# mLSTM gates as 80 rows of one chunk each, and other instruction orders in the MLP and the key projections

## The chip, the cores and the metric

The kernel runs on one core of a Trainium2 chip. A core has five engines that each work through their own instruction stream in order: TensorE (PE, matrix products into eight PSUM banks of 128 x 512 float32), VectorE (DVE), ScalarE (ACT, functions of one operand), GpSimd (POOL) and SyncE (SP), from whose queue this kernel issues all its DMAs. [...] The metric is the device time of one execution in microseconds (us). The profile records one execution with every instruction's start and end; "granted clock" is the share of full speed at which TensorE's clock ran.

## The reference

A two-layer diffusion transformer on 1024 latent tokens of width 1024 and 256 context tokens, all in float32. In both layers each token is normalised (RMS), scaled and shifted by vectors from an AdaLN projection, goes through a mixer and then through an MLP with squared ReLU (width 4096). Layer 0's mixer joins a bidirectional mLSTM of four heads with a windowed attention of eight heads; layer 1's is a grouped-query attention with eight query and two key heads. The part that the change touches most are the mLSTM's gates, for each of 4 heads and 2 directions:

```python
def step(carry, inp):                     # over chunks of 128 tokens
    c_mat, n_vec, m = carry
    qc, kc, vc, ic, fc = inp              # ic input gate, fc log-sigmoid of forget gate
    bcum = jnp.cumsum(fc, axis=-1)
    d_log = jnp.where(lower, bcum[..., :, None] - bcum[..., None, :] + ic[..., None, :], -jnp.inf)
    inter_log = bcum + m[..., None]
    m_t = jnp.maximum(inter_log, jnp.max(d_log, axis=-1))
    inter_w = jnp.exp(inter_log - m_t)
    ...
    w_log = b_last[..., None] - bcum + ic
    m_new = jnp.maximum(b_last + m, jnp.max(w_log, axis=-1))
    carry_w = jnp.exp(b_last + m - m_new)
    w = jnp.exp(w_log - m_new[..., None])
```

The forward direction starts with the two context chunks and goes on with the eight latent ones; the backward direction takes the two context chunks in reverse, then the eight latent chunks in reverse. So there are 2 x 4 x 10 = 80 pairs of a row and a chunk. The running maximum m_t can be had from one scan, m_t = max(m_(t-1) + f_t, i_t), and the cumulative sum from another.

The MLP is `x + gate * (relu(h @ w1) ** 2 @ w2)` for both streams in layer 0, and for the latent tokens alone in layer 1.

## The kernel before, in words

**Number format and products.** Every operand of a large product is split in two parts, a rounded high part ("hi", fp32r) and the rest ("lo"), and a product is three matmuls: hi·hi, hi·lo, lo·hi. `split` (L376 to L379) does this with one copy on ACT and one subtraction on POOL or DVE. A projection of 512 tokens (`proj`, L408) is thus 24 matmuls of 512 columns.

**Who sets the order.** The program is traced in Python order. A planner then orders each engine's instructions: an instruction that its model finds ready goes ahead, earlier traced ones first. Inside `manual_schedule(engines=...)` the named engines keep the traced order. Tiles are recycled; the framework adds the waits that this takes.

**First stage of layer 0** (`first`, L2275, then `mixer0`, L1249). The tokens are normalised and the gate and key projections run as each part becomes ready. `swa_setup` (L1316) copies the gate projection to `gy` (L1329: rows 0 to 3 input gates forward, 32 to 35 input gates backward, 64 to 67 and 96 to 99 the forget gates), projects values (L1330), turns them by TensorE transposes (L1335), and normalises and rotates the keys by `qk_norm` (L470 to L482; single buffers qsq, qt, qsw, qrs). `gates` (L1150 to L1247) follows at once; then the first pair of queries, and seven projections of the gather (L1372 to L1387: mLSTM queries, keys, values, output gates, written to DRAM through the one tile `ev`), which use PSUM banks 6 and 7. Then the window attention (`swa`) with the rest of the gather as filler. Only the mLSTM, later, uses what `gates` returns: `mr` and `ir` (rows of 1280 in high and low parts: the running maximum less the cumulative sum, and the decay), `cb` (the decay of a whole chunk, on all partitions) and `tq` (three values per token, tokens on partitions).

`gates` before works on rows of 1280 tokens: the log-sigmoid on 64 partitions (L1161 to L1168), the backward rows turned around by copies (L1176 to L1182), two scans over 36 x 1280 (L1187, L1188), differences (L1190 to L1200), high and low parts (L1206 to L1210), and for each direction four exponentials into rows of a tile `q` (L1225, L1228), whose last columns are spread to all partitions by matmuls (L1237) and whose ten chunks are transposed (L1242) and copied (L1246).

**The MLP** (`mlp`, L485). Latent products are done by a scheme with seven products in place of eight (sums of blocks of both operands). The first half (`mlp_hidden`, L495) goes over 16 pairs of 128-wide rows of w1. `start` (L661) does pairs 0 and 1 while the normalisation still runs: a list `side` (L677) of steps (normalisation of the second latent group, ten; of the context, `norm_steps`, 17; sums of blocks, four) is advanced by `beside(n)` with counts from `turns` (L713, L734). PSUM banks of a rotating list "A" take the products. `pair` (L775) does one pair: seven products of 12 matmuls, in layer 0 also two context products (`direct`), sums on DVE (`tt`, L624), squared ReLU on ACT (L581, L582), stores to DRAM, and beside it, by `step`, the splits of the next pair's weights (`sums`, L538). In layer 0 `fill(k)` advances the AdaLN projection of layer 1 (`ada_sums`, L195), which sums on DVE (L209, L211) and ends with eight small matmuls (L220). The second half (`mlp_out`, L993) reads the stored sums and w2 in stages "14", "56", "27", "3"; in "14", each step b feeds product 1 (banks 0 to 3) and product 4 (banks 4 to 7). `ahead` (L841) loads and splits its first three steps during the last pair.

After the stages, layer 0 does the context's own second half: 32 steps of twelve matmuls into four banks, four copies on ACT (L1118, L1119), transposes (L1126) and the residual. Then `mixer1` (L1726) loads the weights of the two key heads and of the values, and runs `keys` (L1754: projection; squares and rotation; sum of squares by a matmul at L1772 and root; split) for three token groups and two heads, interleaved by hand (L1817 to L1826).

## Time and profile before

| | |
|---|---|
| median of three runs | 2866.45 us (2858.58 to 2867.11) |
| profiled execution | 2866.29 us, its span 2864.5 us |
| mean granted clock of TensorE | 0.983 |
| TensorE busy | 2733.7 us, 95% of the span |
| DVE, ACT, POOL busy | 1996.7, 1493.8, 1131.6 us |
| DMA | 427.87 MB, 149 GB/s over the span |

How to read the rows of the profile: a row of the waits is "engine, line, waited for: total us, times, longest us". A row of the groups is "line engine operation out<-in count | busy us, mean ns of one | idle us before it <- what ended it". A row of the timeline is "start us, length us, engine line operation", with the idle time before it and what ended it in brackets. A row of the windows is a stretch of the span, its length, the busy time of PE, PEld (TensorE's weight loads), DVE, ACT and POOL with the instructions counted in brackets, the granted clock, the busy share of the DMA engines and GB/s.

### The profile page before, as it was taken

What the parts mean: (1) busy time and instruction counts of PE and PEld (TensorE: products, weight loads), DVE (VectorE), ACT (ScalarE), POOL (GpSimd) and SP (SyncE); (2) the same over time, 40 slices, a digit from 0 to 9 for tenths busy, and PEclk for the clock granted to TensorE, in tenths of its full rate; (3) what the DMA queues carried; (4) which work ended last, traced back from release to release, by engine and by line L of the source; (5) the groups of instructions that cost most, each with busy time, mean ns of one, the idle gap of its engine ahead of it and who ended that gap; (6) DMA issues with size and microseconds to landing.
All of it is one profiled execution on the core that took longest, in us unless ns stands there. A gap on an engine that the chain in (4) does not pass through costs nothing.

```text
span 2864.5 us, 41088 instructions
## 1 busy us (share of the span) xinstructions
PE 2733.7 (95%) x14806; PEld 2314.0 (81%) x14806; DVE 1996.7 (70%) x3289; ACT 1493.8 (52%) x2624; POOL 1131.6 (40%) x748
## 2 busy tenths in 40 slices
PE   6789999999999999989999998999989999999999
PEld 3678788878788878868878888999988888888877
DVE  5836556567868887756777846888885567766766
ACT  5565554444564334334345645888876555444332
POOL 3431221110227666550000335777776398840000
PEclk9989999999999999999999999999999999999999
DMA  6112224252333466669764720100026245577674
GB/s 232 61 48 95 90 88 145 96 199 89 115 103 126 165 209 214 219 209 339 249 213 156 250 88 32 34 19 27 19 83 209 86 158 195 193 254 269 212 229 155
DMA packets 193965, 427.87 MB, mean 149 GB/s; under 512 B 20960, under 2 KB 46688, under 8 KB 193760
## 3 DMA queue, kind: packets, MB, share of 16 engines
q1 hardware_dynamic: 193760, 425.24, 44.7%
q8 instruction: 116, 1.90, 0.3%
q14 instruction: 89, 0.73, 0.1%
HBM read 322.65 MB, written 102.50 MB: 148 GB/s over the span
## 4 chain that ended last, share of the span: by engine, by line
PE 67%; DVE 13%; DMA 7%; issue 5%; ACT 4%; POOL 2%; SPq 0%; DVEq 0%; POOLq 0%; ACTq 0%
PE psum L1020 15%; PE psum L569 15%; PE psum L404 5%; PE psum L406 5%; PE psum L405 5%; PE psum L1955 4%; PE psum L2141 3%; DMA hhiraw<-in_w 3%; PE psum L1861 3%; DVE W L379 2%; PE psum L1111 2%; DVE F L211 2%; DVE F L624 1%; PE psum L1453 1%; POOL W L379 1%
## 5 line engine op out<-in xcount | busy, mean ns | idle before, releaser
L379 POOL TENSOR_TENSOR W<-F,W 128x512 fp32r<-128x512 f32 (+2 forms) x323 | 522.8, 1634 | 507.8 <-ACT W L378 390.7
L1020 PE MATMUL psum<-W,W 128*128 128x512 f32 x2688 | 617.1, 391 | 8.7 <-DVE W L379 5.2
L1020 PEld LDWEIGHTS psum<-W,W 128*128 128x128 f32 x2688 | 503.9, 188 | 121.4 <-DVE W L379 12.6
L569 PE MATMUL psum<-hhi,W 128*128 128x512 f32 (+1 forms) x1600 | 448.7, 360 | 12.8 <-DVE x L624 5.9
L378 ACT ACTIVATE W<-F 128x512 fp32r<-128x512 f32 (+2 forms) x380 | 274.2, 739 | 264.5 <-POOL F L542 96.9
L569 PEld LDWEIGHTS psum<-hhi,W 128*128 128x128 f32 x1600 | 288.9, 191 | 59.1 <-DVE x L624 7.2
L569 PE MATMUL psum<-hlo,W 128*128 128x512 f32 (+1 forms) x800 | 287.2, 359 | 0.0
L378 ACT ACTIVATE W<-hhiraw 128x1024 fp32r<-128x1024 f32 x98 | 104.0, 1061 | 320.9 <-PE psum L1020 247.3
L404 PE MATMUL psum<-hhi,W 128*128 128x512 f32 (+1 forms) x624 | 232.9, 373 | 6.7 <-DVE F L478 6.7
L406 PE MATMUL psum<-hhi,W 128*128 128x512 f32 (+1 forms) x624 | 227.8, 365 | 0.4 <-POOL W L379 0.4
L405 PE MATMUL psum<-hlo,W 128*128 128x512 f32 (+1 forms) x624 | 227.5, 365 | 0.0
L943 DVE TENSOR_TENSOR hhiraw<-hhiraw 128x512 f32<-128x512 f32 x154 | 104.8, 689 | 118.2 <-DMA hhiraw<-in_w 117.4
L542 POOL TENSOR_TENSOR F<-F 128x512 f32<-128x512 f32 x112 | 170.0, 1518 | 20.4 <-DMA F<-in_w 6.9
L569 PEld LDWEIGHTS psum<-hlo,W 128*128 128x128 f32 x800 | 153.3, 192 | 21.8 <-issue 0.2
L372 POOL TENSOR_TENSOR hlo<-F,hhi 128x512 fp32r<-128x512 f32 (+1 forms) x24 | 27.9, 1165 | 358.8 <-ACT F L371 353.7
L379 DVE TENSOR_TENSOR W<-hhiraw,W 128x1024 fp32r<-128x1024 f32 x98 | 119.6, 1221 | 50.0 <-ACT W L378 49.8
L404 PEld LDWEIGHTS psum<-hhi,W 128*128 128x128 f32 x624 | 119.0, 191 | 27.6 <-DVE F L478 7.1
L406 PEld LDWEIGHTS psum<-hhi,W 128*128 128x128 f32 x624 | 118.7, 190 | 17.9 <-POOL W L379 0.8
L405 PEld LDWEIGHTS psum<-hlo,W 128*128 128x128 f32 x624 | 119.2, 191 | 16.9 <-issue 1.7
L569 PE MATMUL psum<-x,W 128*128 128x512 f32 x504 | 123.5, 389 | 0.0
L581 ACT ACTIVATE F<-F 128x512 f32<-128x512 f32 x82 | 51.2, 625 | 134.7 <-DVE F L624 134.7
L379 DVE TENSOR_TENSOR W<-hloraw,W 128x1024 fp32r<-128x1024 f32 x98 | 119.4, 1219 | 1.6 <-ACT W L378 1.6
(435 smaller groups left out, 6471.5 us busy)
## 6 DMA issues: line engine op xcount, KB each, us to landing
F<-in_w SPq DMA_DIRECT2D x104, 512.0 KB, 4.3
hloraw<-hd SPq DMA_DIRECT2D x90, 512.0 KB, 4.8
hhiraw<-in_w SPq DMA_DIRECT2D x72, 512.0 KB, 3.9
hd<-F SPq DMA_DIRECT2D x142, 256.0 KB, 2.1
hhiraw<-in_w SPq DMA_DIRECT2D x116, 256.0 KB, 5.3
F<-in_ada_w SPq DMA_DIRECT2D x96, 256.0 KB, 3.2
hd<-x SPq DMA_DIRECT2D x90, 256.0 KB, 2.4
F<-in_win SPq DMA_DIRECT2D x33, 512.0 KB, 3.7
```

The costliest lines, as they stand in the source:

```text
L378: nc.scalar.activation(hi, src, AF.Copy)
L379: eng.tensor_tensor(lo, src, hi.bitcast(F32), op=ALU.subtract)
L404: nc.tensor.matmul(ps, sh, mh, start=i == 0, stop=False)
L405: nc.tensor.matmul(ps, sh, ml, start=False, stop=False)
L406: nc.tensor.matmul(ps, sl, mh, start=False, stop=i == n - 1)
L542: add = lambda o, p, q, how: nc.gpsimd.tensor_tensor(o, p, q, op=how)
L569: nc.tensor.matmul(ps, w[i][:, p], B[j][k], start=first and j == 0 and m == 0, stop=last and j == 3 and m == 2)
L943: tt = lambda o, p, q, how: eng.tensor_tensor(o, p, q, op=how)
L1020: nc.tensor.matmul(bank(base + i), A[u][:, p], B[v], start=first and m == 0, stop=last and m == 2)
L1861: nc.tensor.matmul(ps, s[:, c], m[:, j, t0 : t0 + QT], start=j == 0 and i == 0, stop=j == ND - 1 and i == 2)
L1955: nc.tensor.matmul(u.o[:, :QT], v[x], p[y], start=c == 0 and m == 0, stop=c == 2 * NB - 1 and m == 2)
L2141: self.nc.tensor.matmul(ps, x[:, c], y, start=first and m == 0, stop=last and m == 2)
```

## The change

**Gates.** The four groups of gate rows are written to DRAM and read back as two tiles of 128 columns (input and forget gates), forward rows as partitions 0 to 39 (head by chunk), backward ones as 64 to 103. Everything then works on 128 columns. Scans run inside each chunk, the backward ones through a reversed view. The sum and the maximum of a whole chunk are one column; a matmul with this column as a broadcast stationary operand and the identity spreads it as a row to all partitions (`across`), where a scan over 80 values, ten per head and direction, carries the maximum from chunk to chunk (the first value of each head is set apart by NEG). It comes back as one column by a product with the identity and a sum along the row, and one more DVE instruction corrects the maxima inside the chunks. `mr` and `ir` go back to rows of 1280 through DRAM; `tq` takes three transposes. The call stands after the first queries and the seven gathered projections. Two tiles of 1280 columns are used where there were six.

```diff
+        gd = dr.tile([4, 4, T], F32, tag="gd", name="gd")
+        for i in range(4):
+            nc.sync.dma_start(gd[i], gy[32 * i : 32 * i + 4, :])
+        for i in range(4):
+            R = (FW, BW)[i % 2]
+            nc.sync.dma_start((ig, y)[i // 2][R, :], gd[i].rearrange("h (c t) -> (h c) t", t=P))
...
+        for R, o in ((FW, slice(None)), (BW, slice(None, None, -1))):
+            nc.vector.tensor_tensor_scan(b[R, o], z[R, :], f[R, o], 0.0, op0=ALU.mult, op1=ALU.add)
+            nc.vector.tensor_tensor_scan(m[R, o], f[R, o], ig[R, o], NEG, op0=ALU.add, op1=ALU.max)
...
+        def across(c):
+            ps = psp.tile("G", "gx")[:, :P]
+            nc.tensor.matmul(ps, col[:, c : c + 1].to_broadcast([P, P]), self.ident, start=True, stop=True)
+            return ps
+        for i, x in enumerate((t, kept)):
+            ps = across(i)
+            nc.vector.tensor_copy(x[:, 0:40], ps[:, 0:40])
...
+        nc.vector.tensor_tensor_scan(t[:, 0:80], t[:, 0:80], kept[:, 0:80], 0.0, op0=ALU.add, op1=ALU.max)
...
+        nc.vector.tensor_tensor(row, row, self.ident, op=ALU.mult)
+        nc.vector.tensor_reduce(c0, row, AX.X, ALU.add)
+        nc.vector.scalar_tensor_tensor(m, b, c0, m, op0=ALU.add, op1=ALU.max)
...
+        nc.scalar.activation(iw, M, AF.Exp, scale=-1.0, bias=c0)
+        nc.scalar.activation(ar, g, AF.Exp, bias=col[:, 3:4])
+        nc.scalar.activation(em, m, AF.Exp, scale=-1.0)
...
+        for i, (x, dst) in enumerate(((Mh, mr), (Ml, mr), (Ih, ir), (Il, ir))):
+            for d, R in enumerate((FW, BW)):
+                w = dr.tile([4, T], F32, tag=f"gd{i}{d}", name=f"gd{i}{d}")
+                nc.sync.dma_start(w.rearrange("h (c t) -> (h c) t", t=P), x[R, :].bitcast(F32))
+                r = 64 * d + 32 * (i % 2)
+                nc.sync.dma_start(dst[r : r + 4, :].bitcast(F32), w)
...
+        for k, x in enumerate((g, ar, em)):
+            nc.tensor.transpose(ps[:, k * P : k * P + P], x, self.ident)
...
-                mr, ir, cb, tq = self.gates(kp, small, psa, gy)
                 for _ in st[-1](psa, 0, qs):
                     pass
...
                 for _ in range(7):
                     next(heads[0])
+                mr, ir, cb, tq = self.gates(kp, small, psa, dr, gy)
```

**Start of the MLP.** `norm_apply` is cut in a first part (scale, shift, high part) and a second (low part). In layer 0 the context's normalisation does the first part of chunk j before the second part of chunk j-1, in 18 steps. The counts of `turns` change, the last context product no longer leaves one drain undone, and the list of banks after the start begins with 4 in layer 0.

```diff
+        for j in range(ND + 1):
+            if j < ND:
+                t.append(self.apply_first(g, ps, layer, which, tp, j, three))
+            if j:
+                self.apply_second(g, layer, which, j - 1, t[j - 1], three)
             yield
...
-                turns = iter((1, 1, 1, 1, 1, 1, 4, 4) if ctx else (0, 1, 1, 2, 1, 2, 1, 2))
+                turns = iter((1, 1, 1, 2, 2, 2, 2, 3) if ctx else (0, 1, 1, 2, 1, 2, 1, 2))
...
-                turns = iter((2, 7, 1, 1) if ctx else (1, 1, 1, 1))
+                turns = iter((4, 6, 1, 1) if ctx else (1, 1, 1, 1))
...
-                        one_left(1)
+                        one_left(int(f < 3))
...
-            psp.tags["A"] = [[0, 1, 2, 3, 4, 5, 6] + ([] if ctx else [7]), 0]
+            psp.tags["A"] = [[4, 5, 6, 0, 1, 2, 3] if ctx else list(range(8)), 0]
```

**End of the first half, start of the second.** In the last pair the AdaLN step moves from behind the first product to behind the third, as in the other pairs. `ahead` loads two steps later where there is a filler. The last two pairs, in both layers, keep the traced order on all engines and on SP. In stage "14" the first two steps are taken together: product 1 of both, product 4 of the first, then (at b = 1) product 4 of the second.

```diff
-            if b == NFF // 2 - 1:
-                fill(2)
...
-            if b < NFF // 2 - 1:
-                fill(3)
+            fill(3)
...
+            if filler:
+                yield
+                yield
             for k in range(2):
                 feed.load(k)
...
-            pair(b, A, nxt)
+            if b < NFF // 2 - 2:
+                pair(b, A, nxt)
+            else:
+                with self.tc.manual_schedule(engines={E.PE, E.DVE, E.Activation, E.Pool, E.SP}):
+                    pair(b, A, nxt)
...
+                if stage == 0 and b < 2:
+                    if b == 0:
+                        first_two = [(*w, e, *queue[e]) for w in plan[kind] for e in range(2)]
+                    queue.popleft()
+                    work = first_two[3:] if b else first_two[:3]
```

**Keys.** The loads and splits of layer 1's first weights are issued from `mlp_out`: those of the keys before the four copies of the context's result, those of the values behind them, with ACT in that order. For each group and head the sum of squares of the group before comes ahead of the next projection; for the context group each head's sum of squares comes ahead of a value product.

```diff
+        wk, wv = self.first_weights
+        wk()
+        with self.tc.manual_schedule(engines={mybir.EngineType.Activation}):
+            for (half, i, k), y in zip(parts, ys):
+                nc.scalar.activation(y, bank(k), AF.Copy)
+            wv()
...
-                    for i in (g, g - 1, g, g - 1):
+                    for i in (g - 1, g, g, g - 1):
                         next(ks[i][kv])
             for kv in range(NKV):
+                next(ks[2][kv])
                 vals(TGS[1], (kv,))
-                for _ in range(2):
-                    next(ks[2][kv])
+                next(ks[2][kv])
```

More of the change, by code (lines that the diff above doesn't have):

```diff
@@ L858, in ahead @@
             yield
-            yield
-            yield
+            if not filler:
+                yield
+                yield
             for k in (1, 2):
@@ L1079, in mlp_out @@
                     both = kind == "3"
-                    first = b == 0 and not (both and half == R)
+                    first = b + e == 0 and not (both and half == R)
                     last = b + e == ns - 1 and not (both and half == L)
@@ L1117, in mlp_out @@
         ys = cuts(F, H, *(3 * PG + i * H for i in range(4)))
-        for (half, i, k), y in zip(parts, ys):
-            nc.scalar.activation(y, bank(k), AF.Copy)
+        wk, wv = self.first_weights
[4 more added lines that the diff above has]
+            wv()
         for j, k in zip(range(0, ND, 2), (5, 2, 7, 6)):
@@ L1140, in norm_steps @@
         yield
-        for j in range(ND):
-            self.norm_apply(g, ps, layer, which, tp, [j], three)
+        if layer:
+            for j in range(ND):
+                self.norm_apply(g, ps, layer, which, tp, [j], three)
+                yield
+            return
+        t = []
+        for j in range(ND + 1):
[3 more added lines that the diff above has]
+                self.apply_second(g, layer, which, j - 1, t[j - 1], three)
             yield
@@ L1213, in gates @@
[L1213 removed]
         tq = cbt.tile([P, 2, NT, 12], F32, tag="tq")
+        ps = across(4)
         for d in range(2):
[L1216 to L1246 removed]
@@ L1723, in residual, with begin_mixer1, keys, vals @@
         self.nc.vector.scalar_tensor_tensor(xs, ps[:, :n], gate, xs, op0=ALU.mult, op1=ALU.add)
+    def begin_mixer1(self):
+        a, wp = self.a, self.weights_ring((4, 5, 0, 1), (PG, 2 * PG, 0, 0))
+        self.wk, self.wv = [], []
+        def keys():
+            self.wk += [self.unit(wp, a["win1"][8 + kv]) for kv in range(2)]
+        def vals():
+            self.wv += [self.unit(wp, a["wv1"][:, i * 1024 : i * 1024 + 1024]) for i in range(2)]
+        self.first_weights = keys, vals
     def mixer1(self, xd, side):
```

176 lines of the change are left out of this document (76 added, 100 removed).

## The prediction

> **What bounds the kernel now.** I read the page's busy times first, then TensorE's waits, then windows and timelines around each long wait.
>
> ```profile
> span 2864.5 us, 41088 instructions
> PE 2733.7 (95%) x14806; PEld 2314.0 (81%) x14806; DVE 1996.7 (70%) x3289; ACT 1493.8 (52%) x2624; POOL 1131.6 (40%) x748
> ```
>
> TensorE (PE) is the bound: 2864.5 - 2733.7 = 130.8 us of the span is all that it idles. An edit that leaves its matmuls as they are can win only some of that idle time, and the slow clock that follows it. So the question for each edit is which PE wait it touches (columns: total, times, longest):
>
> ```profile
> PE psum L220 <- DVE F L211: 12.9, 3, 8.5
> PE psum L404 <- DVE F L478: 6.7, 1, 6.7
> PE psum L569 <- DVE x L624: 5.9, 3, 3.1
> PE psum L569 <- ACT F L581: 5.4, 1, 5.4
> PE psum L1772 <- DVE F L465: 4.6, 2, 3.1
> PE psum L1126 <- ACT F L1119: 4.4, 1, 4.4
> PE psum L1242 <- issue: 4.3, 1, 4.3
> PE psum L404 <- DVE F L1775: 3.6, 1, 3.6
> PE psum L1020 <- ACT F L581: 2.0, 1, 2.0
> PE psum L1413 <- DVE small L1246: 1.6, 1, 1.6
> PE psum L1020 <- DVE x L624: 1.2, 1, 1.2
> ```
>
> Windows around them (window, then its length, then busy time of PE, PEld, DVE, ACT, POOL, then the granted clock, DMA share, GB/s) price the waits with the clock:
>
> ```profile
> 92.50:191.00 98.50, 80.74 (x374) 64.75 (x374) 64.79 (x83) 61.47 (x94) 40.15 (x26) 0.88 0.16 52
> 93.00:147.00 54.00, 42.96 (x193) 34.14 (x192) 53.31 (x54) 34.57 (x52) 23.58 (x15) 0.91 0.17 55
> 142.00:146.00 4.00, 4.00 (x10) 3.13 (x11) 3.94 (x4) 3.89 (x6) 2.53 (x2) 0.50 0.25 99
> 872.00:876.00 4.00, 3.76 (x9) 2.99 (x10) 4.00 (x4) 3.43 (x9) 4.00 (x4) 0.50 0.05 6
> 1152.00:1156.00 4.00, 4.00 (x12) 3.15 (x13) 3.20 (x5) 2.18 (x4) 2.23 (x2) 0.66 0.98 334
> 1230.00:1252.00 22.00, 13.53 (x51) 10.96 (x50) 16.04 (x19) 10.13 (x19) 11.27 (x9) 0.77 0.56 180
> 1268.00:1282.00 14.00, 10.82 (x40) 8.18 (x39) 7.17 (x6) 7.09 (x11) 8.58 (x4) 0.88 0.99 367
> 1676.00:1680.00 4.00, 3.87 (x20) 3.74 (x21) 3.25 (x7) 1.86 (x5) 1.53 (x1) 0.63 0.38 95
> 1746.00:1750.00 4.00, 3.29 (x17) 3.29 (x18) 1.04 (x3) 0.42 (x1) 0.00 (x0) 0.65 0.29 114
> 2500.00:2555.00 55.00, 55.00 (x244) 45.43 (x243) 34.29 (x40) 26.55 (x41) 39.47 (x24) 1.00 0.61 202
> ```
>
> After a wait of some microseconds PE runs about 4 us at a clock of 0.5 to 0.66: 1.4 to 2 us more are lost. In the gates' stage VectorE (DVE) is busy 53.31 of 54 us. There, DVE and not PE sets the pace.
>
> **Part 1, the gates.** 92.5 is where the gate projections end, 191 where the first attention scores start. PE's work between them, at full clock, is about 80.74 x 0.88 = 71 us. The gates' own forms of that window:
>
> ```profile
> L1242 PE MATMUL psum<-ident,x 128*128 128x128 f32 x20 | 4.1, 354 | 4.3 <-issue 4.3
> L1237 PE MATMUL psum<-x,ident 128*128 128x10 f32 x16 | 2.8, 308 | 0.2 <-ACT x L1228 0.2
> L1165 DVE SCALAR_TENSOR_TENSOR x<-x,x 64x1280 f32<-64x1280 f32 x1 | 3.5, 3487 | 0.1
> L1187 DVE TENSOR_TENSOR_SCAN x<-s6f,x 36x1280 f32<-36x1280 f32 x1 | 2.8, 2817 | 0.0
> L1246 DVE COPY small<-psum 128x16 f32<-128x16 f32 x12 | 1.3, 166 | 0.6 <-PE psum L1242 0.6
> L379 DVE TENSOR_TENSOR VV<-psum,VV 128x128 fp32r<-128x128 f32 x2 | 0.6, 282 | 0.0
> L1182 DVE COPY x<-s6f 4x256 f32<-4x256 f32 x1 | 0.3, 283 | 0.0
> L1225 ACT ACTIVATE x<-x 4x1280 f32<-4x1280 f32 x4 | 5.1, 1266 | 7.0 <-DVE x L1188 7.0
> L1206 ACT ACTIVATE s6f<-x 4x256 f32<-4x256 f32 x1 | 0.4, 413 | 0.0
> ```
>
> Removed on DVE: 23 such forms (L1164 to L1246; the costliest and the last stand above), 40.7 us by their busy column. Removed on ScalarE (ACT): the forms L1161 to L1230, 22.8 us, first and last by size above. PE loses 36 instructions, 4.1 + 2.8 = 6.9 us, and gets three broadcast products and three transposes, 6 x 0.354 = 2.1 at most. Rows 1280 long become 128 long, so the new gates have about 48 DVE instructions between 0.166 and 0.282 us: 8 to 14, I take 11 (the scan, 2817/10 = 0.28, agrees with the upper row). ACT: nine of about 0.3, 3 us. Net relief: DVE 30 us, ACT 20, PE 5.
>
> [...]
>
> What this frees: L478 at 141.4 is what PE waits for 6.7 us, because the next gathered projection needs bank 6, which the last K tile holds, and L478 stands behind L1187, L1188, L1190, L1191, L1196 and L1200 on DVE. Without these six forms, none longer than L1187's 2.8 us, it comes up to 17 us sooner, before PE gets there. The wait at L1242 (4.3) and the one at L1413 (1.6, scores behind the gates' copies in bank 5) belong to the old gates. So the stage can shrink from 98.5 to 71 - 5 = 66 us and a little more: 32 us at best. What is late next: the K and Q chains through single buffers qsq, qt, qrs, whose POOL and ACT parts stay; and PE's own waits for the new gates, whose products are strung between DVE steps. PE has seven gathered projections to fill with. Bounds: 10 (only the named waits, 12.6, less some) and 28; I take **19**, nearer the upper, since DVE's saturation is the plain cause.
>
> Its DMAs: 24 on SP (4 + 4 in, 8 + 8 out), in write-read pairs through DRAM, among the gather's weight loads and stores.
>
> ```profile
> u<-F SPq DMA_DIRECT2D x16, 128.0 KB, 1.7
> ACT F L1381 <- DMA u<-F: 9.8, 3, 7.0
> 2554.68 25.55 PE L1020 MATMUL psum<-W,W 128*128 128x512 f32 x112
> ```
>
> Each read waits for its write, by the row 1.7 us; behind it on SP stand the stores u<-F, and for these waits ACT with its one tile ev. mr and ir themselves aren't read before the mLSTM. Cover: two PSUM banks of gather, two projections of 24 matmuls at 25.55/112 = 0.228, 5.4 us each. I cost them at nothing while SP is held for less than that at a time; more is the third rival.
>
> **Part 2, start of layer 0's MLP.** The 5.4 us wait for L581 is bank 0, still held by the context's first tile, whose drain stands behind the group sums on ACT:
>
> ```profile
> 860.89 0.68 DVE L624 TENSOR_TENSOR F<-psum,F 128x512 f32<-128x512 f32 x1
> 871.83 0.36 ACT L581 ACTIVATE F<-psum 128x256 f32<-128x256 f32 x1
> 872.24 0.80 PE L569 MATMUL psum<-hhi,W 128*128 128x512 f32 x1 [5.45 <-ACT F L581]
> ```
>
> The new order of banks starts with 4, drained at 861.6 by L624, then 5 and 6; bank 0 comes three products (8 us) later. The turns, the step-ahead in the normalisation and the empty drain list move work earlier: 32 steps in place of 31, no new instruction. Worth 5.45 + half of 3.76 = 7.3 at most, 3 if DVE (busy 4 of 4 us there) makes the later products wait; I take **6**.
>
> **Part 3, end of that MLP's first half.** The longest wait, 8.47 us before L220, is the last AdaLN product standing behind the pair's first product while L211 on DVE is unfinished; it moves two products (2 x 12 matmuls, 5.4 us) later, and the last two pairs follow program order, where L211 stands in the pair before it. The feed's first loads come two steps later in the pair, behind the filler whose tiles they overwrite. Then 2.0 + 1.2 at L1020 for banks 4 to 7: the second half now issues product 1 of both first steps (banks 0 to 3) before product 4 (banks 4 to 7), which gives 2.7 us more. By the windows, 22 - 13.53 + clock 2.5 = 11, and 3.2 + 1.3 = 4.5. Bounds 5 (3 us left at L220, and operands of the second step late, wanted 2.7 us earlier than before) and 15.5; I take **11**.
>
> **Part 4, the keys' start.**
>
> ```profile
> 1674.05 1.06 ACT L378 ACTIVATE W<-F 128x1024 fp32r<-128x1024 f32 x1 [5.20 <-DMA F<-in_wv]
> 1675.01 2.04 ACT L1119 ACTIVATE F<-psum 128x512 f32<-128x512 f32 x4
> ```
>
> L1119's copies stand behind a split that waits for its DMA; the change puts them first. Saved 4.4 + 0.37 x 3.87 = 5.8, less half a microsecond of copying; but the split of the values' second weights comes later, perhaps just when wanted: 3 to 5.8, **5**. The other orders put each key's sum of squares before the next projection, so L465 frees the bank a projection (5.4, or 2.7 for the context) earlier: waits 4.6 and 3.6, clock 1.1, so 2 to 9.3; I take **6**, as the last wait depends on the ones before.
>
> **What may come in.** In layer 1 the last two pairs get the same fixed order, SP included, where PE idles not at all (55.00 of 55.00): nothing to win, 0 to 10 us to lose, if the second half's loads stand on SP behind writes that wait for DVE. Elsewhere the planner's order shifts. Waits of the kind of L569 <- L624 (5.9 in three) can come or go: -2 to 6. Together I take **6 lost**, 2 of them clock. [...]
>
> **Sum.** 19 + 6 + 11 + 5 + 6 = 47, less 6: 41. The profiled execution took 2866.29 us (span 2864.5 and 1.8 around it), which is the median of the three runs, 2866.45, within 0.2. So 2866.3 - 41 = **2825 us**; its own range, with every term halfway to its bounds, 2812 to 2842.
>
> **Rivals.**
> *A new wait for the old one.* PE works in order, and a broadcast product placed before its DVE chain is ready holds all gathered projections behind it. For it: L1242 <- issue and L404 <- L478 are such waits in the same stage. Against: the chain has 30 us less of DVE work. Priced like the old ones: 12.6 of wait and two slow stretches of 2, 17 us: 2842 to 2850, say 2845.
> *All of it.* Every term at its upper bound, 28 + 7.3 + 15.5 + 5.8 + 9.3 = 66, nothing new: 2800.
> *SP held, slower than before.* If the planner puts the gates' 16 last DMAs ahead of the gather's stores, SP holds for the gates' chain (57 short ops of about 0.25, 14 us) and twelve writes to land (12 x 1.7 = 20) and their issue, 40 us; the two banks cover 11, PE stands 29 and some 8 at half clock, 33 in all, and the stage's 19 are gone: 2866 - 22 + 33 = 2877. It decides from 33 us of hold. Against: stores that are ready can stand between the pairs.
> *It doesn't do what it says.* Outside the fixed stretches the planner orders by readiness, and could leave the gates where they were and lose elsewhere what the orders win: 2862.
>
> **Chances.** Forecast 0.58; new wait 0.20; all 0.10; SP 0.06; no effect 0.06. A measurement of this kernel tells 0.3%, 8.6 us, from no change. Faster 0.87 (the first three, less a tail of the second), same 0.07, slower 0.06. The range must take in the second and third case: 2799 to 2854 leaves out SP, no effect and small tails.
>
> **What would show it.** Right: DVE no longer near 10 of 10 between 93 and 147; L404 <- L478 gone; first scores near 172 and not 191; no wait before the second pair's first product; L220's longest under 3 us; L1126 <- L1119 under 1. Wrong: PE waits in the new gates' products above 5 us together, ACT waiting for u<-F above 15, PE idle between 2500 and 2570, or L1020 waiting in either layer.

## The result and the profile after

The changed kernel takes 2832.19 us (median; 2831.75 to 2833.66 over four runs), the kernel before 2864.67 (2858.58 to 2867.11): a ratio of 0.9892, 95% interval 0.9877 to 0.9906, or 32.5 us less. The prediction was 2825, 41 us less. The profiled execution took 2831.75 us with a span of 2830.0, 34.5 less than the span before. Its page and its longest PE waits after the start-up (columns as before):

```profile
span 2830.0 us, 41032 instructions
...
PE 2725.0 (96%) x14779; PEld 2305.7 (81%) x14779; DVE 1952.3 (69%) x3296; ACT 1476.0 (52%) x2611; POOL 1119.5 (40%) x743
```

```profile
PE psum L1039 <- POOL W L392: 8.4, 4, 3.5
PE psum L582 <- DVE x L637: 7.9, 5, 3.1
PE psum L220 <- DVE F L211: 6.9, 4, 3.7
...
PE psum L1039 <- ACT W L391: 4.1, 1, 4.1
```

The lines have moved: L220 stays, L378/L379 are now L391/L392, L404 L417, L465 L478, L478 L491, L569 L582, L624 L637, L1020 L1039, L1126 L1154, L1772 L1822. (Line 478 of before and L478 here are not the same.) The waits behind the old gates (6.7, 4.3, 1.6), at the start of the MLP (5.4) and before the key transposes (4.4) are gone. In their place stand 12.5 us at L1039, the products of the MLP's second half, where before there were 3.2 outside DVE's steady splits.

Where the time went can be read from PE waits that both traces have at the same place of the program. Timeline of PE (start, duration, instruction, and the wait ahead of it), before:

```profile
212.18 0.39 PE L1459 MATMUL psum<-x,VV 128*128 128x256 f32 x1 [0.98 <-ACT x L378]
...
771.36 0.33 PE L1640 MATMUL psum<-ident,hhis 128*128 128x128 f32 x1 [0.55 <-DVE hhis L1637]
...
1069.03 0.80 PE L569 MATMUL psum<-hhi,W 128*128 128x512 f32 x1 [3.09 <-DVE x L624]
...
1766.84 0.70 PE L1872 MATMUL psum<-F,ones 128*128 128x256 f32 x2 [1.25 <-ACT F L1869]
...
2238.84 0.47 PE L569 MATMUL psum<-hhi,W 128*128 128x512 f32 x1 [0.94 <-DVE x L1723]
```

and after:

```profile
185.28 0.38 PE L1498 MATMUL psum<-x,VV 128*128 128x256 f32 x1 [0.86 <-ACT x L391]
...
747.68 0.33 PE L1679 MATMUL psum<-ident,hhis 128*128 128x128 f32 x1 [0.55 <-DVE hhis L1676]
...
1038.26 0.79 PE L582 MATMUL psum<-hhi,W 128*128 128x512 f32 x1 [3.09 <-DVE x L637]
...
1727.09 0.70 PE L1922 MATMUL psum<-F,ones 128*128 128x256 f32 x2 [1.25 <-ACT F L1919]
...
2198.03 0.47 PE L582 MATMUL psum<-hhi,W 128*128 128x512 f32 x1 [0.94 <-DVE x L1762]
```

| stretch | lead at its end | gained in it | predicted |
|---|---|---|---|
| to the attention's start (gates) | 212.18 - 185.28 = 26.9 | 26.9 | 19 |
| attention and mLSTM | 771.36 - 747.68 = 23.7 | -3.2 | in the 6 lost |
| start and first half of layer 0's MLP | 1069.03 - 1038.26 = 30.8 | 7.1 | 6 |
| border of the halves, second half, copies, keys | 1766.84 - 1727.09 = 39.8 | 9.0 | 11 + 5 + 6 = 22 |
| rest of layer 1's mixer | 2238.84 - 2198.03 = 40.8 | 1.0 | 0 |
| layer 1's MLP, to the end of the span | 2864.5 - 2830.0 = 34.5 | -6.3 | in the 6 lost |

So the sum came out near its forecast by two errors that cancel in part: the gates won 8 us more, the stretch with the border 13 less. Each row compares one execution of each kernel, and equal work scatters between executions. From the attention's start to the mLSTM's end the changed kernel took 562.4 us and the kernel before 559.2, but nine kernels of the experiments below with the same instructions there took 559.4 to 561.7; so on the average only 1.3 of the 3.2 us are lost there. In the same way the start and first half of layer 0's MLP took 290.5 to 293.4 us in the eight traces with the changed start that show the wait at its end, and 296.2 to 297.7 in the four with the old start: 5 us on the average, and not 7.1. Windows of the changed kernel over the gates' stage, layer 0's border and what follows layer 1's wait of 3.19 (window, length, busy time of PE, PEld, DVE, ACT, POOL, granted clock, DMA share, GB/s):

```profile
92.50:164.50 72.00, 68.19 (x335) 55.44 (x334) 29.73 (x60) 40.01 (x76) 34.61 (x23) 0.98 0.23 73
93.00:147.00 54.00, 50.19 (x242) 39.97 (x241) 29.33 (x56) 36.59 (x70) 30.43 (x22) 0.97 0.21 65
1230.00:1252.00 22.00, 12.97 (x43) 9.58 (x42) 9.17 (x6) 9.70 (x14) 15.32 (x8) 0.77 0.69 230
2517.70:2520.70 3.00, 2.98 (x10) 2.37 (x11) 2.18 (x2) 1.30 (x2) 1.83 (x2) 0.73 0.89 341
2520.70:2524.00 3.30, 3.30 (x12) 2.63 (x11) 0.00 (x0) 0.70 (x1) 3.30 (x2) 0.73 0.88 280
```

In the gates' stage DVE is busy 29.33 of 54 us, where it was 53.31, and the stage lasts 72 us in place of 98.5: PE idles 3.8 us instead of 17.8 (14 won), its clock is 0.98 and not 0.88 (68.19 us of busy time at 0.88 in place of 0.98 would be 76: some 8 won), and it has about 4 us less to do. The stretch with the long waits of layer 0's border, now at 1230 to 1252 (the same times as before, but some 30 us later in the program), looks like the old one did: 12.97 of 22 us busy at a clock of 0.77 (13.53 and 0.77 before).

### The profile page after: what moved, and what is told of

Read it like the earlier page. It is cut to its first block, busy times and chain, and to the rows that moved or that the text cites. A ratio compares the mean times of both kernels' runs of the same rounds, so it can differ in the third digit from the quotient of the medians.

```text
span 2830.0 us, 41032 instructions
## 1 busy us (share of the span) xinstructions
PE 2725.0 (96%) x14779; PEld 2305.7 (81%) x14779; DVE 1952.3 (69%) x3296; ACT 1476.0 (52%) x2611; POOL 1119.5 (40%) x743
## 4 chain that ended last, share of the span: by engine, by line
PE 57%; DVE 13%; DMA 8%; issue 6%; POOL 3%; ACT 3%; SPq 0%; DVEq 0%; POOLq 0%; ACTq 0%
PE psum L582 11%; PE psum L1039 11%; DMA hhiraw<-in_w 5%; PE psum L417 4%; PE psum L419 4%; PE psum L418 4%; PE psum L2005 4%; PE psum L2191 3%; PE psum L1135 3%; DVE W L392 3%; PE psum L1911 3%; POOL W L392 2%; DVE F L637 2%; DVE x L211 1%; DVE F L211 1%
## 5 line engine op out<-in xcount | busy, mean ns | idle before, releaser
L392 POOL TENSOR_TENSOR W<-F,W 128x512 fp32r<-128x512 f32 (+2 forms) x323 | 519.0, 1622 | 544.3 <-ACT W L391 433.8
L1039 PE MATMUL psum<-W,W 128*128 128x512 f32 x2688 | 618.9, 392 | 16.0 <-POOL W L392 8.4
L1039 PEld LDWEIGHTS psum<-W,W 128*128 128x128 f32 x2688 | 506.4, 189 | 128.2 <-POOL W L392 10.2
L582 PE MATMUL psum<-hhi,W 128*128 128x512 f32 (+1 forms) x1600 | 448.8, 360 | 9.7 <-DVE x L637 7.9
L391 ACT ACTIVATE W<-F 128x512 fp32r<-128x512 f32 (+2 forms) x380 | 273.4, 739 | 267.0 <-POOL F L555 97.1
L582 PEld LDWEIGHTS psum<-hhi,W 128*128 128x128 f32 x1600 | 288.9, 192 | 56.7 <-DVE x L637 8.0
L582 PE MATMUL psum<-hlo,W 128*128 128x512 f32 (+1 forms) x800 | 287.1, 359 | 0.0
L391 ACT ACTIVATE W<-hhiraw 128x1024 fp32r<-128x1024 f32 x98 | 103.8, 1061 | 309.8 <-PE psum L1039 208.4
L417 PE MATMUL psum<-hhi,W 128*128 128x512 f32 (+1 forms) x624 | 232.8, 373 | 0.0
L582 PEld LDWEIGHTS psum<-hlo,W 128*128 128x128 f32 x800 | 153.4, 192 | 21.8 <-issue 0.2
L392 DVE TENSOR_TENSOR W<-hhiraw,W 128x1024 fp32r<-128x1024 f32 x98 | 119.7, 1222 | 65.1 <-ACT W L391 63.8
L417 PEld LDWEIGHTS psum<-hhi,W 128*128 128x128 f32 x624 | 118.6, 190 | 20.3 <-ACT x L391 2.5
L594 ACT ACTIVATE F<-F 128x512 f32<-128x512 f32 x82 | 51.3, 625 | 139.0 <-DVE F L637 138.8
L392 DVE TENSOR_TENSOR W<-hloraw,W 128x1024 fp32r<-128x1024 f32 x98 | 119.6, 1220 | 5.8 <-ACT W L391 5.8
L582 PE MATMUL psum<-x,W 128*128 128x512 f32 x504 | 123.5, 389 | 0.0
```

The lines of the kernel that those rows point to most:

```text
L391: nc.scalar.activation(hi, src, AF.Copy)
L392: eng.tensor_tensor(lo, src, hi.bitcast(F32), op=ALU.subtract)
L417: nc.tensor.matmul(ps, sh, mh, start=i == 0, stop=False)
L582: nc.tensor.matmul(ps, w[i][:, p], B[j][k], start=first and j == 0 and m == 0, stop=last and j == 3 and m == 2)
L1039: nc.tensor.matmul(bank(base + i), A[u][:, p], B[v], start=first and m == 0, stop=last and m == 2)
```

## The experiments

Twelve kernels ran. Each edit is against the changed kernel unless said otherwise; "border" is the place where the MLP's second half starts. A ratio is to the kernel before, timed alongside, with its 95% interval.

### SP left out of the fixed order

```diff
-with self.tc.manual_schedule(engines={E.PE, E.DVE, E.Activation, E.Pool, E.SP}):
+with self.tc.manual_schedule(engines={E.PE, E.DVE, E.Activation, E.Pool}):
```

> The changed kernel, with one edit: in the last two pairs of each layer's MLP the fixed order holds for PE, DVE, ACT and POOL, and SP (the queue that issues the DMAs) is left to the planner, as before the change. Theory A, SP's fixed order makes the second half's operands late: its loads were issued only at 1228.65, behind stores that wait for DVE, and POOL waited 11.1 us for them; then the waits of 4.10, 3.45 and 1.47 us at L1039 in layer 0 and of 3.19 in layer 1 go, 12.2 us and some clock, less the old waits of the same place that may return (2.0 + 1.2): 2818 to 2824 us, from 2832.2. Rival B, the loads' place in the program (two steps later than before) makes them late: 2832 plus or minus 2, with the L1039 waits as they are. Rival C, the new order of the first two steps wants the second step's operands 2.7 us sooner: 2832 plus or minus 2 too.

Measured 2832.0 us (2827.94 to 2835.16), ratio to before 0.9884 (0.9859 to 0.9909): no change. Theory A falls: the first loads were issued at 1204.88 in place of 1228.65, but the waits stayed, also in layer 1 (timeline of PE, then of POOL in layer 1):

```profile
1229.79 0.50 PE L1039 MATMUL psum<-W,W 128*128 128x512 f32 x1 [1.95 <-ACT W L391]
...
1234.04 5.49 PE L1039 MATMUL psum<-W,W 128*128 128x512 f32 x12 [3.75 <-POOL W L392]
...
1242.04 18.21 PE L1039 MATMUL psum<-W,W 128*128 128x512 f32 x72 [2.51 <-POOL W L392]
...
2515.12 15.08 PE L1039 MATMUL psum<-W,W 128*128 128x512 f32 x58 [3.15 <-POOL W L392]
```

```profile
2509.68 5.38 POOL L392 TENSOR_TENSOR W<-F,W 128x1024 fp32r<-128x1024 f32 x2 [3.69 <-ACT W L391]
```

### No fixed order

```diff
-if b < NFF // 2 - 2:
+if b < NFF // 2:
     pair(b, A, nxt)
```

> The changed kernel without the fixed order: the last two pairs of each MLP are ordered by the planner on every engine, as before the change; all else as changed. Theory A (SP's fixed order makes the operands late): the L1039 waits go, 12.2 us and some clock; but the fixed order also brought the longest wait at L220 down from 8.47 to 1.99 us, and if that hangs on the order, 6.5 us come back: 2820 to 2830. Rival B or C (late by place in the program, or wanted too soon): the waits stay, and L220's comes back too: 2834 to 2842. If L220 stays near 2 us, the moved filler steps alone brought it down.

Measured 2824.22 us (2823.43 to 2828.01), ratio 0.9860 (0.9836 to 0.9884): all four runs are below all four of the changed kernel, by 8 us in the median. So the fixed order costs, as theory A had it for the time, but not where it had it: layer 1's border has no wait left over 0.4 us, while layer 0's waits add up to what they were (12.0 against 12.4 us, each wait over 0.4 counted), with another end:

```profile
1205.87 0.50 PE L582 MATMUL psum<-hhi,W 128*128 128x512 f32 x1 [2.24 <-DVE x L637]
...
1230.21 0.50 PE L1039 MATMUL psum<-W,W 128*128 128x512 f32 x1 [1.98 <-ACT W L391]
...
1232.64 2.50 PE L1039 MATMUL psum<-W,W 128*128 128x512 f32 x5 [1.93 <-POOL W L392]
...
1240.42 1.65 PE L1039 MATMUL psum<-W,W 128*128 128x512 f32 x3 [5.28 <-ACT F L594]
...
1242.59 17.61 PE L1039 MATMUL psum<-W,W 128*128 128x512 f32 x65 [0.52 <-DVE x L637]
```

L220 has no wait over 0.4 us at the border here: the moved filler steps, and not the fixed order, brought its wait down.

### The second half's first loads at their old place

```diff
-if filler:
-    yield
-    yield
 for k in range(2):
     feed.load(k)
```

(and two empty steps after the first split, as before the change)

> The changed kernel with the second half's first loads put two steps earlier in layer 0's last pair, where they stood before the change (the fixed order stays, SP included). Theory B, their place makes them late: issued 5.4 us sooner, the operands come 5 us sooner, and of the 9.0 us of waits at L1039 in layer 0 5 to 8 go: 2824 to 2828. Theory A, SP is held by stores that wait for DVE: standing two steps earlier they pass some of the stores, but they must wait for the filler that still reads their tiles, and the AdaLN loads stand behind them: 2829 to 2836, with a longer wait at L220. Layer 1 (no filler) isn't touched and keeps its 3.19 us by either.

Measured 2839.26 us (2838.44 to 2840.29), ratio 0.9910 (0.9887 to 0.9933): 7 us slower by the medians, 5 by the ratios. The filler now runs two products later than it did before the change, so these loads overwrite a tile from which it still has to take its sums, and the last AdaLN values that this kernel computes are not the reference's. PE shows it, as the product of the filler waits for the load:

```profile
1228.73 1.84 PE L220 MATMUL psum<-ones,F 128*128 128x2 f32 x8 [18.28 <-DMA F<-hd]
```

It does not decide theory B. It shows that the two steps of delay belong to the filler's new place: the tiles come free later, and so must the loads.

### The second half's first two steps in their old order

```diff
-if stage == 0 and b < 2:
+if stage == 0 and b < 0:
```

> The changed kernel with the second half's first two steps in their old order (product 1 and then product 4 of the first step, then the second step), in both layers. Theory C, the new order wants the second step's operands 2.7 us sooner than they can be there: the waits for splits at L1039 shrink by 2 to 5 us in layer 0 and to nothing in layer 1 (3.19), while the waits for banks 4 to 7 (2.0 and 1.2 before) come back in layer 0: 2826 to 2830. Theory A or B (operands late for another cause): layer 0's waits for the first step stay at 4 to 6 us, bank waits come on top: 2831 to 2836.

Measured 2833.42 us (2832.33 to 2836.48), ratio 0.9893 (0.9865 to 0.9921): no change. Theory C falls: L1039 waits 5.83 + 3.46 + 1.68 us in layer 0, 2 more than with the new order, and 1.19 + 2.83 in layer 1.

### POOL left out of the fixed order

```diff
-with self.tc.manual_schedule(engines={E.PE, E.DVE, E.Activation, E.Pool, E.SP}):
+with self.tc.manual_schedule(engines={E.PE, E.DVE, E.Activation, E.SP}):
```

> The changed kernel with POOL taken out of the fixed order of the last two pairs (PE, DVE, ACT and SP keep it). Theory P: the fixed order strings on POOL, for each step of the second half, an addition (L962, 1.3 us) that ACT's splits wait for, and two subtractions (L392, 2.4 us each) that wait for ACT; the next step's addition stands behind them, so a step takes 8 us (POOL at 1235.61, 1243.57, 1251.59) where PE needs 5.4 for its 24 products. With POOL free the additions go first, as before the change, and the waits at L1039 shrink from 12.2 us to 6 or less: 2823 to 2828. Rival Q (the operands are late because the tiles they go into, or the DMAs, are late, whatever POOL's order): 2830 to 2834, with layer 1's 3.2 us as it is.

Measured 2831.52 us (2831.26 to 2833.13), ratio 0.9893 (0.9871 to 0.9914): no change, rival Q's number. POOL does change its order, as theory P wanted, but its first addition still waits for a load that SP issues late, and layer 1's wait is 3.20. Timeline of POOL in this kernel, in layer 1:

```profile
2500.17 1.28 POOL L962 TENSOR_TENSOR F<-F 128x512 f32<-128x512 f32 x1 [5.65 <-DMA F<-in_w]
2502.62 2.41 POOL L392 TENSOR_TENSOR W<-F,W 128x1024 fp32r<-128x1024 f32 x1 [1.17 <-ACT W L391]
2504.99 1.28 POOL L962 TENSOR_TENSOR F<-F 128x512 f32<-128x512 f32 x1
```

and in the changed kernel:

```profile
2501.84 1.29 POOL L962 TENSOR_TENSOR F<-F 128x512 f32<-128x512 f32 x1 [6.04 <-DMA F<-in_w]
2504.30 4.75 POOL L392 TENSOR_TENSOR W<-F,W 128x1024 fp32r<-128x1024 f32 x2 [1.17 <-ACT W L391]
2509.01 1.30 POOL L962 TENSOR_TENSOR F<-F 128x512 f32<-128x512 f32 x1
```

### The fixed order on PE and DVE alone

```diff
-with self.tc.manual_schedule(engines={E.PE, E.DVE, E.Activation, E.Pool, E.SP}):
+with self.tc.manual_schedule(engines={E.PE, E.DVE}):
```

> The changed kernel with the fixed order of the last two pairs kept on PE and DVE alone; ACT, POOL and SP are left to the planner. Theory S (the operands of the second half pass SP, POOL and ACT in a row, and each fixed order holds them by itself, which is why freeing SP or POOL alone won nothing): with all three free it is near the kernel without any fixed order, 2822 to 2827, and layer 1's wait of 3.2 us at L1039 is gone. Rival T (PE's or DVE's fixed order is what costs): 2829 to 2834, with that wait in place.

Measured 2825.74 us (2823.89 to 2830.82), ratio 0.9865 (0.9847 to 0.9883): the time that theory S gives, and rival T falls. Layer 1's border has no wait, and POOL's additions there start at 2484.30 in place of 2501.84 (PE is 1.4 us ahead at that time), both ahead of the second half's subtractions (128x1024):

```profile
2484.30 1.29 POOL L962 TENSOR_TENSOR F<-F 128x512 f32<-128x512 f32 x1 [1.87 <-DMA F<-in_w]
...
2487.10 1.29 POOL L962 TENSOR_TENSOR F<-F 128x512 f32<-128x512 f32 x1 [0.26 <-DMA F<-in_w]
2489.56 2.42 POOL L392 TENSOR_TENSOR W<-F,W 128x1024 fp32r<-128x1024 f32 x1 [1.17 <-ACT W L391]
```

The operands pass SP (load), POOL (add), ACT (high part) and POOL (low part). Freed alone, SP or POOL wins nothing; all three free, the wait is gone. ACT alone was not tried, so these runs don't tell a chain of three held links from ACT as the only one. The 3.69 us for which POOL waited for ACT with SP free speak for ACT as the link that held there. POOL's addition had ended at 2506.00, but ACT took the split at 2508.56, in the traced order behind L594, which itself waited for DVE (ACT, SP left out of the fixed order):

```profile
2506.17 0.63 ACT L594 ACTIVATE F<-F 128x512 f32<-128x512 f32 x1 [4.14 <-DVE F L637]
...
2508.56 1.99 ACT L391 ACTIVATE W<-F 128x1024 fp32r<-128x1024 f32 x2
```

### Everything at the border as before the change

The edits of the second and fourth experiment together, with the loads at their old place and the filler's steps back at theirs, so that they no longer collide:

```diff
 prod(ps, A["11"], B11)
+if b == NFF // 2 - 1:
+    fill(2)
 nc.scalar.activation(t, ps, AF.Copy)
...
 prod(ps, A["12"], B21)
-fill(3)
+if b < NFF // 2 - 1:
+    fill(3)
```

> The changed kernel with everything at the border between the two halves of the MLP put back as it was before: no fixed order, the filler's steps and the second half's first loads at their old places, the first two steps in their old order. The gates, the start of layer 0's MLP, the copies and the keys stay changed. If the border's edits win 11 us as predicted, this is slower than the changed kernel by 11 in layer 0, less what they cost in layer 1: 2836 or more. If, as the trace reads, the wait at L220 was only swapped for later operands (1 us net in layer 0) and layer 1 lost 5 by the fixed order, this is 3 to 6 us faster than the changed kernel: 2825 to 2830.

Measured 2825.27 us (2824.31 to 2831.01), ratio 0.9864 (0.9847 to 0.9882): 7 us faster than the changed kernel in the median, and the same as without the fixed order (2824.22). The edits at the border together cost 7 us, where I had them at 11 won and layer 1's order at no more than a part of the 6 lost; without the fixed order the rest of them wins 1 us, which is within the noise. The trace is of the slowest of the four runs (2831.01). In it L220 waits long again, and the total is the old one (12.9 with one wait of 0.52 that is not shown):

```profile
1211.46 1.87 PE L220 MATMUL psum<-ones,F 128*128 128x2 f32 x8 [7.24 <-DVE F L211]
...
1244.26 1.65 PE L1038 MATMUL psum<-W,W 128*128 128x512 f32 x3 [5.14 <-ACT F L594]
```

### The second operand's low parts on DVE

Against the kernel without the fixed order:

```diff
-feed.split_b(0, eng)
+feed.split_b(0, nc.vector)
...
-feed.split_b(k, eng)
+feed.split_b(k, nc.vector)
```

> The changed kernel without the fixed order, and with the low parts of the second operand (split_b) of the first three steps of the second half, in both layers, computed on DVE (1.22 us for 128x1024 in the trace) in place of POOL (2.4 us). If POOL's time is what PE still waits for at L1039 in layer 0 (1.93 us and part of the 5.28 after it), it is 2 to 4 us faster than without the fixed order alone: 2820 to 2823. If the operands are late because their tiles or DMAs are (ACT waited 5.0 us for F from hd), nothing changes: 2824 plus or minus 2; and slower, 2826 or more, if the splits hold up DVE's own work on the last pair.

Measured 2831.43 us (2827.70 to 2832.26), ratio 0.9877 (0.9860 to 0.9894): 7 us slower by the medians, 5 by the ratios, than with POOL. The third case of the expectation: DVE's own work on the last pair comes later, and with it the banks that PE wants (L637 finishes the pair):

```profile
1237.59 1.62 PE L1039 MATMUL psum<-W,W 128*128 128x512 f32 x3 [4.58 <-DVE x L637]
...
1242.95 1.65 PE L1039 MATMUL psum<-W,W 128*128 128x512 f32 x3 [3.74 <-DVE F L637]
```

### The new gates alone

The kernel before with the new gates (the new function, with the pool for its DRAM tiles as an argument) at their new place, all other edits left out.

```diff
-mr, ir, cb, tq = self.gates(kp, small, psa, gy)
...
 for _ in range(7):
     next(heads[0])
+mr, ir, cb, tq = self.gates(kp, small, psa, dr, gy)
```

> The kernel before with the new gates alone, at their new place (after the first steps of the gather); all other edits left out. Theory W (the old gates' long rows on DVE set the pace of that stage): the first scores move 27 us forward as in the changed kernel, two or three are lost again in attention and mLSTM: 23 to 25 us faster than before, 2838 to 2842 us. Rival: the 27 us need the other edits to reach the end (the queue orders behind move as well): less than 15 us faster, over 2848.

Measured 2835.94 us (2833.09 to 2841.63), ratio 0.9909 (0.9887 to 0.9930), by the ratio 26 us less than before: theory W, 1 us past its range. The lead at the attention's start is 25.9 us (186.27 against 212.18). In this kernel the wait before the key transposes (4.4 at L1126 of before) is absent although its copies were left as they were; with the old gates moved (next experiment) it is there, with 3.6 us.

### The old gates at the new place

The kernel before, its function for the gates unchanged, called later.

```diff
-mr, ir, cb, tq = self.gates(kp, small, psa, gy)
...
 for _ in range(7):
     next(heads[0])
+mr, ir, cb, tq = self.gates(kp, small, psa, gy)
```

> The kernel before with its old gates, rows of 1280 as they are, called at the new place, after the first steps of the gather. Theory W: DVE has the same 41 us of work in the same stretch or carries it on into the attention's start, whose own work it delays: between 8 us faster and 10 slower, 2855 to 2875 us. Rival L (the place in the order is what wins: DVE takes the gather's steps first and the old gates' products no longer hold PE): 15 to 25 us faster, 2838 to 2848.

Measured 2857.34 us (2847.81 to 2863.36 over ten runs), ratio 0.9978 (0.9964 to 0.9992): 6 us less than before, within theory W's range and at its better end. DVE stays busy for 51.91 of the 54 us, with the long rows in it:

```profile
93.00:147.00 54.00, 44.25 (x205) 34.22 (x204) 51.91 (x54) 35.24 (x57) 25.89 (x16) 0.94 0.17 59
```

### The new gates at the old place

The kernel before, with the new function called where the old one was.

```diff
-mr, ir, cb, tq = self.gates(kp, small, psa, gy)
+mr, ir, cb, tq = self.gates(kp, small, psa, dr, gy)
```

> The kernel before with the new gates called at the old place, ahead of the attention's last set-up and of the gather. Theory W (the form decides): within 4 us of the kernel with the new gates at their new place, so 20 us or more faster than before. Rival L (the place decides): less than 10 us faster, 2853 or more, since PE waits in the new gates' products or SP in their write-read pairs (for both of which the trace would have rows at L1234, L1280 and ACT waiting for u<-F).

Measured 2842.1 us (2838.47 to 2845.36), ratio 0.9927 (0.9907 to 0.9948): 21 us less than before. The form wins 21, the place 6, and both together 26: within the intervals (up to 6 us either way) they add up. DVE's busy time in the window falls with the form:

```profile
93.00:147.00 54.00, 49.20 (x240) 38.71 (x238) 33.86 (x86) 36.46 (x73) 28.95 (x20) 0.97 0.18 55
```

### The key steps in their old order

```diff
-for i in (g - 1, g, g, g - 1):
+for i in (g, g - 1, g, g - 1):
...
-    next(ks[2][kv])
     vals(TGS[1], (kv,))
-    next(ks[2][kv])
+    for _ in range(2):
+        next(ks[2][kv])
```

> The changed kernel with the order of the key steps (in layer 1's mixer) put back as it was before; the copies and the value weights keep their new order. By the prediction's term this costs 6 us (2 to 9): 2834 to 2838, with waits near 3.1 and 3.6 us at the sums of squares and at the next projection. By the changed kernel's trace, which kept one wait of 3.47 there, the order won 3 to 5: 2835 to 2837. If those waits were going to be hidden or moved anyway: 2832 plus or minus 1.5.

Measured 2838.88 us (2833.59 to 2840.78), ratio 0.9904 (0.9888 to 0.9920): slower than the changed kernel by 6.7 us in the medians and 3.4 by the ratios. In the traces, from the first wait at L1822 to the end of the one at L1922, the keys last 1733.5 - 1691.0 = 42.5 us here and 1727.1 - 1690.4 = 36.7 in the changed kernel: 5.8 us. The old wait at the next projection (3.6) is back. This term was right: its three measures, 3.4 to 6.7 us, lie within the bounds of 2 to 9.3.

## Why the prediction was right, and where it was not

**The total** lies 7 us above the forecast, within its own range, and in the direction forecast.

**The gates (19 taken, 10 to 28).** The mechanism was right and the size too small: 26.9 us at the attention's start (25.5 to 29.4 in the nine traces with the same gates), 26 alone at the end. What failed is the choice of 19. My own working gave 66 us of PE's work for a stage of 98.5, "32 at best", and I stayed halfway because the K and Q chains through single buffers might have come late next; all of PE's idle time in that stage is 3.8 us. What I had put at nothing, the DMAs on SP, did cost nothing: PE has no wait at the new products, and in the gates' stage ACT waited 0.3 us for the gather's stores. The 11 us for the new instructions on DVE held within their 8 to 14: the rows of the changed kernel that belong to the gates (48 instructions, with the fills and the two splits; three of the rows below) add up to 12.1. L1218, over 128 columns, took 0.29 us; more than half of the instructions (29) are narrower, most of them 0.145 (L1264) to 0.2.

```profile
L1224 DVE TENSOR_TENSOR_SCAN x<-x 40x128 f32<-40x128 f32 x2 | 0.8, 412 | 0.0
...
L1218 DVE TENSOR_TENSOR x<-x 128x128 f32<-128x128 f32 x1 | 0.3, 291 | 0.0
...
L1264 DVE COPY gcol<-x 40x1 f32<-40x1 f32 x1 | 0.1, 145 | 0.0
```

Form and place, which I did not part, are 21 and 6 us. The fall of DVE's busy time with the form, and its 51.91 of 54 us with the old form at the new place, show the mechanism.

**The start of the MLP (6).** 7.1 us in its stretch and some 5 on the average of the traces, within the bounds of 3 to 7.3; there is no wait before the second pair's first product, and in the two kernels with the new gates and the old start it is there with 5.2 us. No run has this edit alone.

**The border (11, 5 to 15.5).** This is the step that failed: it won 1 us in layer 0 by the medians, and nothing for certain, and cost some 6 in layer 1. I read 8.47 us at L220 and 3.2 at L1020 as two waits that an order can remove, and summed them. As far as the runs show, they are stations of one stretch that takes its time: the waits over 0.4 us of layer 0's border add up to 8.7 to 14 us in every kernel but the one whose loads overwrite the filler's tile (11.6 before, 12.4 changed, 8.7 with SP free, 12.0 and 8.7 without the fixed order and with it on PE and DVE alone, 12.9 with the old border, 13.5 with splits on DVE), whichever instruction they stand at. Moved from L220, the wait came back at the first operands. The bounds held the cause by name, "operands of the second step late, wanted 2.7 us earlier than before", but as something that costs 6 us at most, and the lower bound of 5 should have been 0 or below. The trace of before already spoke against the second part. The wait at L1020 for banks 4 to 7 had its cause a step further up: the split on ACT ahead of L581 was held by its load (ACT and SP, before):

```profile
1270.27 1.06 ACT L378 ACTIVATE W<-F 128x1024 fp32r<-128x1024 f32 x1 [4.42 <-DMA F<-hd]
```

```profile
1266.31 0.32 SPq L898 DMA_DIRECT2D F<-hd  x1
```

What sets the length of that stretch is not settled. The loads write tiles that the last pair and the filler still use, which would make them late whatever the order; no run tried other tiles.

**What may come in (6 lost).** Right in size and named at the right place: layer 1's fixed order cost 3.19 us of wait at 2514.5 and 0.27 x 6.3 = 1.7 of clock after it. Layer 1's MLP, to the end of the span, takes 630.8 to 635.0 us in the six traces that fix ACT's order and 625.4 to 627.8 in the eight that leave ACT, POOL and SP free. Wrong, or at least not enough, is the cause I gave, loads on SP behind writes: SP free alone changes nothing, and the wait is gone in the runs that free SP, POOL and ACT together. Of the 3.2 us lost in attention and mLSTM, most is scatter.

**Copies (5) and keys (6).** The wait of 4.4 at L1126 is gone, but it was gone too with the new gates alone, so what the edit itself wins is open. The keys measured 5.8 in the traces.

**The rivals.** A new wait for the old one came, but at the border and not at the gates' products; the gates' rival and SP held are refuted by the rows above (no wait at L1234 or L1282). Of the signs named for a right step all came but one: L220's longest wait is 3.66 us, at another place of that MLP, and 1.99 at the border (the first scores moved to 191 - 26.9 = 164, not 172). Of those for a wrong step two came, a wait between 2500 and 2570 and waits at L1020's successor in both layers, and both point to the border.

## What to carry to other kernels

A row count can cost more than the arithmetic: the same gates as 80 rows of 128 instead of 36 rows of 1280 freed an engine that paced a stage (DVE, busy 53.31 of 54 us before and 29.33 after), and won most of the stage's idle time (14 of 17.8 us) with the clock's loss on top. Waits at neighbouring instructions of one border aren't to be summed as if each could go alone; ask first whether a chain through several engines sets the border's length, and try the edits together and apart. A hand-written order that fixes every engine also fixes the queues that only feed; here leaving it out, or keeping it on two engines, is 6 to 8 us faster than the changed kernel (2824 to 2826 us).

## What the hardware showed that was not expected

**After waits of PE of 1.89 to 3.4 us the clock went either way.** In the fourteen traces I took every wait of PE over 1.2 us, from 30 us on, that stands alone (no other wait over 0.4 us in the 5 us before it or the 2.5 after), and the granted clock in the 2.5 us after it: 204 waits, many of them at the same places of different kernels. After waits of up to 1.5 us the clock was full (0.97 or more) in 37 of 38, and in 45 of 54 from there to 1.85; from 1.89 to 3.4 us it was at 0.8 or lower after 47 of 80 and full after 26; from 3.45 us on it was at 0.76 or lower after all 32. The same wait at the same place did either: at L488 near 122 us, waits of 1.91 to 1.97 us were followed by a clock of 0.52 to 0.62 in seven kernels and of 1.00 in four. Windows in the changed kernel after waits of 1.93, 3.47 and 3.12 us:

```profile
122.80:125.30 2.50, 2.50 (x4) 1.33 (x5) 2.28 (x9) 2.43 (x6) 1.47 (x2) 0.52 0.00 0
1693.80:1696.30 2.50, 2.47 (x9) 2.32 (x10) 1.73 (x3) 0.60 (x2) 0.00 (x0) 0.50 0.00 0
1121.90:1124.40 2.50, 2.50 (x8) 2.03 (x9) 2.43 (x4) 2.26 (x4) 0.65 (x1) 0.72 0.97 326
```

and in the kernel with the old key order, after 1.95 and 3.12 us at the first and the last of these places of the program:

```profile
122.10:124.60 2.50, 2.48 (x13) 1.91 (x14) 2.28 (x9) 2.43 (x6) 1.40 (x2) 1.00 0.00 0
1122.50:1125.00 2.50, 2.50 (x11) 2.09 (x12) 2.43 (x4) 2.25 (x4) 0.66 (x1) 1.00 0.96 320
```

What decides between a full clock and a low one is not shown by these runs. Between 2 and 3.3 us the clock was at 0.8 or lower after 38 of 57 waits. From this, and from the prediction's windows of 4 us at 0.5 to 0.66, I would price such a wait, as an estimate, at a chance of two in three of 1.4 to 2 us more.

**The short scan took more than its share of the long one.** 1280 columns took 2.817 us (L1187 of before) and 128 took 0.412 (L1224). By these two, as an estimate, a column takes 2.09 ns and 0.145 us stand beside, as much as a copy of one column took (L1264); the scan of 80 columns (L1247) took 0.315 where this gives 0.312. I had scaled it by columns alone, to 0.28.
